# Order of the k and q products, the way to the triangular inverses, and the squares of q in a gated DeltaNet layer

## The chip, the core and the metric

The kernel runs on one core of one Trainium2 chip, in one launch. The metric is the device time of that launch in microseconds (us), median of three runs. The core's engines run at the same time, each through its own list of instructions in a fixed order, and wait for one another by semaphores: TensorE (PE in the profile; PEld is its loading of weights) multiplies into PSUM, VectorE (DVE) and ScalarE (ACT) work element by element, GpSimd (POOL) does a few odd operations, and SyncE (SP) issues most of the DMA transfers.

## The reference

One layer on x of shape (1, 256, 2048), float32. It has two parallel token mixers behind one input projection, an output projection, and a gated MLP.

```python
h = rmsnorm(x, norm_mix_w)
q, k, v, z, b_raw, a_raw, p_in, g_a, g_b = split(h @ w_in)
q, k, v = split(silu(causal_dwconv(concat([q, k, v]), conv_qkv_w)))   # 4 taps
q = l2norm(q per head) * HEAD_DIM ** -0.5;  k = l2norm(k per head)    # 16 heads of 128
o = gated_delta_rule(q, k, v, g_log, beta)                            # chunks, triangular solve
y_a = rmsnorm(o, gdn_norm_w) * silu(z)
y_b = (causal_multiscale_pool(p_in) @ pool_w per group) * pool_scale
x = x + (sigmoid(g_a) * y_a + sigmoid(g_b) * y_b) @ w_out
h = rmsnorm(x, norm_ffn_w)
gate, up = split(h @ w_up)
x = x + (gelu(causal_dwconv(gate, conv_ffn_w) + conv_ffn_b) * up) @ w_down
return rmsnorm(x, norm_final_w)
```

l2norm divides by the root of a sum of squares over a head's 128 channels. The kernel leaves q unscaled in the products and brings the sum of squares of q into the final scale of o: that is what "squares of q" means below.

## The kernel before

**Long products.** Every big product is float32, made of three products of rounded parts: a weight tile `raw` of 128 x 1024 comes by DMA; ScalarE rounds it to the high half `whi` (line 141 of the listing, L141), VectorE subtracts to get the low half `wlo` (L149); `gemm_a` (L168) then issues, for each of two rows of 128 inputs and each of two halves of the 256 tokens, x-high by `whi` (L179), x-low by `whi` (L180) and x-high by `wlo` (L181). Each of these is a product 128 x 512. A projection of 512 columns takes 8 weight tiles, 96 such products. `raw` has four buffers, `whi` and `wlo` three each, and weights are made two tiles ahead (`AHEAD`). The result stands in PSUM in a tile of the pool `psm`, which has two buffers; other PSUM tiles come from `psg`, with four.

**Groups.** The mixers run over four groups g of 512 columns, that is four heads. Before the change a group issues its long products in this order: k, q, v, p (input of the pool), g_b, the pool's small product (24 products), z, g_a. The eight weight streams are listed in the same order in `srcs`. The very first k product is done apart, while x is still being loaded.

**What follows each product.** `evict` (L552) scales the PSUM tile into `ev` on ScalarE (L557, two instructions); `ev` has one buffer. `conv_silu` (L597) turns `ev` with eight small TensorE products (`turned`, L224), scales on ScalarE (L608), adds three shifted taps on VectorE (L611), and applies silu (L614, L615) into `kq`. v goes out to DRAM (`vrow`), and comes back three times shifted as `mv`; VectorE multiplies with the taps and adds (L588, L589). The gates are a tanh on ScalarE (L871) that VectorE combines with z (L882, L884, L886). Such work is put in the list `later`, which is emptied at the second weight tile of the next long product.

**The gated delta rule.** `gdn` (L619) is a generator. After each six long products `side()` takes one step of it, so its small instructions are put between the long ones. It makes the products of k and q with themselves and their decays (L645 to L683), sends the diagonal blocks of 32 through DRAM (`cdd`) into `lb` so that all blocks can be inverted side by side, idles for `WAIT` = 5 steps, and inverts them by forward substitution on VectorE (L709 to L711, 31 steps, in `tb`). The inverses go back through DRAM (`tbd`) into `TT`, are turned by blocks (L730), and are joined into larger inverses (L743 to L772). Then come the recurrence over the chunks (L778 to L789), the outputs (`po`: L796, L798, L799), the squares of q summed by 16 products with q's squares as weights and a column of ones (L804, waited for by L812), the squares of o (L809, L810), the power on GpSimd (L814), and the scaled output (L816, L819). `gated` multiplies it with z and adds the pool's part (L890, L891), `mixed` turns the result and splits it into halves for the output projection (L903, L904).

**Order.** A scheduler places the instructions on each engine from the program order, its estimate of when operands and buffers are free, and priorities; each engine then works strictly through its list. Two places are tied by hand (`issue_after`, at the first group). The lists of the changed program can be read as well as those of the program before: where the text says "in the changed order", it is from them.

Of the kernel before, what the change touches and what calls it, by code (L numbers as in the profile page):

```python
# [7 lines left out]
F32 = mybir.dt.float32  # L8
F32R = mybir.dt.float32r
I32 = mybir.dt.int32  # L10
AF = mybir.ActivationFunctionType
ALU = mybir.AluOpType

P = 128
S = 256
D = 2048
NH = 16
KD = D // P
DFF = 5632
KF = DFF // P  # L20
EPS = 1e-6
# [3 lines left out]
C_Q, C_K, C_V, C_Z = 0, 2048, 4096, 6144  # L25
C_B, C_P, C_GA, C_GB = 8192, 8224, 10272, 12320
B0 = 32
NR = P // B0
AHEAD = 2
WAIT = 5  # L30


@with_exitstack
def kernel(
# [20 lines left out]
    nc = tc.nc  # L55
    mm = nc.tensor.matmul
# [10 lines left out]
    def nm(s):  # L67
        cnt[0] += 1
        return f"{s}_{cnt[0]}"

    def pg(shape=(P, 512)):
        return psg.tile(list(shape), F32, tag="g", name=nm("psg"))


    def cols(w, base, nk):
        return [w[c * 256 : (c + 1) * 256, base : base + 512].rearrange("(k p) f -> p k f", p=P)
                for c in range(nk // 2)]

    srcs = []
    for g in range(4):  # L80
        for base in (C_K, C_Q, C_V, C_P, C_GB):
            srcs += cols(w_in[0], base + 512 * g, KD)
            if g == 0 and base == C_K:
                srcs += [w_in[0, c * 1024 : (c + 1) * 1024, C_B : C_B + P].rearrange("(k p) f -> p k f", p=P)
                         for c in range(2)]
        srcs += cols(pool_w[0, g], 0, 4)
        for base in (C_Z, C_GA):
            srcs += cols(w_in[0], base + 512 * g, KD)
    outw = [cols(w_out[0], 512 * c, KD) for c in range(4)]
# [76 lines left out]
    later = []  # L166
# [62 lines left out]
    ones = cpool.tile([P, P], F32, name="ones")  # L229
    nc.gpsimd.memset(ones, 1.0)  # L230
    ident = cpool.tile([P, P], F32, name="ident")
# [17 lines left out]
    mp = mix.__enter__()  # L249
# [183 lines left out]
    for cq in range(4):  # L433
        pr = slice(32 * cq, 32 * cq + 32)
# [17 lines left out]
    nc.vector.tensor_tensor(id2, ident[:64, 0:32], ident[:64, 32:64], op=ALU.add)  # L452


    pba = pg([P, 2, S])
    for c in range(2):
        hi, lo = weights()
        for kk in range(8):
            k = 8 * c + kk
# [137 lines left out]
    def conv_silu(e, kind, g, dst):  # L597

        pts = turned(e)
        y = mp.tile([P, 4, S], F32, tag="cy", bufs=2, name=nm("cy"))  # L600
        for f in range(4):
            r = kind * 16 + 4 * g + f
            gs = pts[f // 2][:, f % 2, :]

            def w(j):
                return cqw[:, j * 48 + r : j * 48 + r + 1]

            nc.scalar.activation(y[:, f, :], gs, AF.Copy, scale=w(3))  # L608
            for j in (2, 1, 0):
                s = 3 - j  # L610
                nc.vector.scalar_tensor_tensor(y[:, f, s:], gs[:, : S - s], w(j), y[:, f, s:],  # L611
                                               op0=ALU.mult, op1=ALU.add)
        th = mp.tile([P, 4, S], F32, tag="th", name=nm("th"))
        nc.scalar.activation(th, y, AF.Tanh)  # L614
        k_conv.append(nc.vector.scalar_tensor_tensor(dst, th, 1.0, y, op0=ALU.add, op1=ALU.mult).ins)  # L615
# [3 lines left out]
    def gdn(g, kq, vt, conv, res):  # L619
# [79 lines left out]
        for cq in range(4):  # L699
            nc.sync.dma_start(lb[32 * cq : 32 * cq + 32], cdd.rearrange("q (r j) i -> (q r) j i", j=B0))  # L700
        yield
        for _ in range(WAIT):
            yield
        tb = mp.tile([P, 8, B0], F32, tag="tb", name=nm("tb"))
        tmp = mp.tile([P, 8, B0], F32, tag="tmp", name=nm("tmp"))
        nc.vector.tensor_copy(tb, idb)
        for j in range(B0 - 1):
# [15 lines left out]
        for h in range(4):  # L723
            for t in range(2):
                nc.scalar.activation(vt[:, t, h, :], vt[:, t, h, :], AF.Copy, scale=nk[:, t, h : h + 1])
        for _ in range(WAIT - 3):
            yield
        for r in range(NR):
            rs = slice(B0 * r, B0 * (r + 1))
            nc.vector.transpose(Ta[rs, :, rs], TTa[rs, :, rs])  # L730
# [50 lines left out]
        pr = pg([P, 4, P])  # L781
# [6 lines left out]
            mm(pw[:, h, :], TT[h // 2][:, 1, h % 2, :], vt[:, 1, h, :], start=True, stop=True)  # L788
        nc.scalar.copy(w2, pw)  # L789
        yield  # L790

        q2 = kq[:, :, 1, :]
        nc.scalar.activation(q2, q2, AF.Square)
        po = [pg([P, 4, P]) for t in range(2)]
        for h in range(4):
            mm(po[0][:, h, :], ga0[:, h, 256:384], w1[:, h, :], start=True, stop=True)  # L796
# [1 line left out]
            mm(po[1][:, h, :], ga0[:, h, 384:512], w1[:, h, :], start=True, stop=False)  # L798
            mm(po[1][:, h, :], ga1[:, h, P : 2 * P], w2[:, h, :], start=False, stop=True)  # L799
        yield  # L800
        pn = pg([P, 2, 4])
        for t in range(2):
            for h in range(4):
                mm(pn[:, t, h : h + 1], q2[:, h, t * P : (t + 1) * P], ones[:, 0:1], start=True, stop=True)  # L804
        ro = mp.tile([P, 2, 4], F32, tag="ro", name=nm("ro"))
        so = mp.tile([P, 2, 4], F32, tag="so", name=nm("so"))
        for t in range(2):
# [1 line left out]
            nc.scalar.activation(o2, po[t], AF.Square, scale=float(P) ** -0.5)  # L809
            nc.vector.tensor_reduce(so[:, t, :], o2, axis=mybir.AxisListType.X, op=ALU.add)  # L810
        yield
        nc.vector.tensor_scalar(ro, pn, EPS * P, EPS * EPS * P, op0=ALU.mult, op1=ALU.add)  # L812
        nc.vector.tensor_tensor(ro, ro, so, op=ALU.add)
        nc.gpsimd.tensor_tensor(ro, ro, epsx[:, 0:1].unsqueeze(2).to_broadcast([P, 2, 4]), op=ALU.pow)  # L814
        for t in range(2):
# [4 lines left out]
        yield  # L820
        res.append(on)

    for g in range(4):
        kq = mp.tile([P, 4, 2, S], F32, tag="kq", bufs=1, name=nm("kq"))
        for kind, dst in ((1, kq[:, :, 0, :]), (0, kq[:, :, 1, :])):
            ps = ps_k0 if kind == 1 and g == 0 else gemm_a(xh, xl, KD)
            e = evict(ps)
            later.append(lambda e=e, kind=kind, g=g, dst=dst: conv_silu(e, kind, g, dst))

        vt = mp.tile([P, 2, 4, P], F32, tag="vt", name=nm("vt"))  # L830
        vt2 = vt.rearrange("p t h d -> p t (h d)")
        res = []
        later.append(lambda g=g, kq=kq, vt=vt, res=res: side_work.__setitem__(0, gdn(g, kq, vt, v_conv(g, vt), res)))
        v_taps(g)
        if g == 0:
            def after_k(k_conv=k_conv[0]):
                with tc.issue_after(last_pow[0]), tc.issue_after(k_conv):
                    fixed_parts()

            later.append(after_k)  # L840
        e = evict(gemm_a(xh, xl, KD), rsh)
        nc.sync.dma_start(vrow[g, SH : SH + S, :].rearrange("(t p) d -> p t d", p=P), e)
        later.append(lambda e=e, g=g, vt2=vt2: v_moved(e, g, vt2))


        win = WINDOWS[g]
        psb = scales(g)
        ps = gemm_a(xh, xl, KD)
        e = evict(ps)
        phi = mtile(g, [P, 4, S], F32R, nm("phi"))  # L850
        plo = mtile(4 + g, [P, 4, S], F32R, nm("plo"))

        def pooled(e=e, g=g, phi=phi, plo=plo):
            for f2 in range(2):
                pt = pg([P, 2, S])
                for ff in range(2):
                    fs = slice((2 * f2 + ff) * P, (2 * f2 + ff + 1) * P)
                    mm(pt[:, ff, P:S], e[:, 1, fs], bands[:, g, P + PAD : NB], start=True, stop=False,
                       skip_group_check=True)
                    mm(pt[:, ff, 0 : P + PAD], e[:, 0, fs], bands[:, g, 0 : P + PAD], start=False, stop=True,  # L860
                       skip_group_check=True)
                fs = slice(2 * f2, 2 * f2 + 2)
                nc.scalar.copy(phi[:, fs, :], pt)
                nc.vector.tensor_tensor(plo[:, fs, :], pt, phi[:, fs, :].bitcast(F32), op=ALU.subtract)

        later.append(pooled)

        def gate(ps, tag):
            th = mp.tile([P, 2, 512], F32, tag=tag, name=nm("gate"))
            for t in range(2):  # L870
                nc.scalar.activation(th[:, t, :], ps[:, t, :], AF.Tanh, scale=rsh[:, t : t + 1])  # L871
            return th

        tb = gate(gemm_a(xh, xl, KD), "th")
        ps = gemm_a(lambda k, t: phi[:, k, t * P : (t + 1) * P], lambda k, t: plo[:, k, t * P : (t + 1) * P], 4)
        yb = mp.tile([P, 2, 512], F32, tag="yb", name=nm("yb"))
        nc.vector.tensor_tensor(yb, ps, psb.unsqueeze(1).to_broadcast([P, 2, 512]), op=ALU.mult)
        nc.vector.scalar_tensor_tensor(yb, tb, 1.0, yb, op0=ALU.add, op1=ALU.mult)

        ps = gemm_a(xh, xl, KD)  # L880
        sz = mp.tile([P, 2, 512], F32, tag="sz", name=nm("sz"))
        nc.vector.scalar_tensor_tensor(sz, gate(ps, "th"), 1.0, ps, op0=ALU.add, op1=ALU.mult)  # L882
        ta = gate(gemm_a(xh, xl, KD), "th")
        nc.vector.scalar_tensor_tensor(sz, ta, 1.0, sz, op0=ALU.add, op1=ALU.mult)  # L884
        sz4 = sz.rearrange("p t (h d) -> p (t h) d", h=4)
        nc.vector.tensor_tensor(sz4, sz4, gwb.unsqueeze(1).to_broadcast([P, 8, P]), op=ALU.mult)  # L886

        def gated(sz=sz, res=res, yb=yb):
            drain()
            nc.vector.tensor_tensor(sz, res[0].rearrange("p t h d -> p t (h d)"), sz, op=ALU.mult)  # L890
            nc.vector.tensor_tensor(sz, sz, yb, op=ALU.add)  # L891

        if g < 3:
            gated()
        mh = mtile(g, [P, 4, S], F32R, f"mhi{g}")
        ml = mtile(4 + g, [P, 4, S], F32R, f"mlo{g}")
        mhi.append(mh)
        mlo.append(ml)

        def mixed(sz=sz, mh=mh, ml=ml):  # L900
            for f2, pt in enumerate(turned(sz)):
                fs = slice(2 * f2, 2 * f2 + 2)
                nc.scalar.copy(mh[:, fs, :], pt)  # L903
                nc.vector.tensor_tensor(ml[:, fs, :], pt, mh[:, fs, :].bitcast(F32), op=ALU.subtract)  # L904

        if g < 3:
            later.append(mixed)
# [174 lines left out]
```

## Time and profile before

| | us |
|---|---|
| median of three runs | 1575.46 (1575.41 to 1575.91) |
| the profiled execution | 1577.65 |
| its span, first to last instruction | 1575.9 |
| mixer, four groups of about 177 us each | from about 36 to 744 |
| output projection, MLP, final norm | from about 744 on |

The profile's rows give a start, a duration, the engine, the line, the operation, the names `out<-in` and shapes; `xN` says how many instructions a row holds. In square brackets stands the idle time of the engine ahead of the row and what ended it. Durations of products overlap, as TensorE is pipelined: what a product costs is the distance between two starts. In tables by line, the columns after the shapes are the busy time in us, the mean of one in ns, and the idle time of the engine ahead of these instructions. In the list of waits, a row names who waited for whom: us in total, how often, and the longest.

### The profile page before, as it was taken

What the parts mean: (1) busy time and instruction counts of PE and PEld (TensorE: products, weight loads), DVE (VectorE), ACT (ScalarE), POOL (GpSimd) and SP (SyncE); (2) the same over time, 40 slices, a digit from 0 to 9 for tenths busy, and PEclk for the clock granted to TensorE, in tenths of its full rate; (3) what the DMA queues carried; (4) which work ended last, traced back from release to release, by engine and by line L of the source; (5) the groups of instructions that cost most, each with busy time, mean ns of one, the idle gap of its engine ahead of it and who ended that gap; (6) DMA issues with size and microseconds to landing.
All of it is one profiled execution on the core that took longest, in us unless ns stands there. A gap on an engine that the chain in (4) does not pass through costs nothing.

```text
span 1575.9 us, 21328 instructions
## 1 busy us (share of the span) xinstructions
PE 1563.6 (99%) x8078; PEld 1314.0 (83%) x8078; DVE 1067.4 (68%) x1625; ACT 745.1 (47%) x956; POOL 45.1 (3%) x69
## 2 busy tenths in 40 slices
PE   9999999999999999999999999999999999999997
PEld 8877888788878888788888888888888888888886
DVE  6897848795788757796555667766766677444544
ACT  6554436444545445444454544444444445334443
POOL 2110000000000000000000000000000000000000
PEclk9999999999999999999999999999999999999999
DMA  8676757676667756666566666666666666666662
GB/s 274 196 227 188 203 147 214 191 218 170 184 203 200 204 147 201 198 209 178 191 197 184 189 188 187 187 188 188 186 191 191 190 188 207 199 196 205 202 222 92
DMA packets 168230, 304.23 MB, mean 193 GB/s; under 512 B 19235, under 2 KB 22835, under 8 KB 167999
## 3 DMA queue, kind: packets, MB, share of 16 engines
q1 hardware_dynamic: 165104, 297.84, 63.7%
q10 hardware_dynamic: 3022, 5.03, 1.0%
q8 instruction: 63, 1.03, 0.3%
q14 instruction: 41, 0.33, 0.1%
HBM read 297.56 MB, written 5.27 MB: 192 GB/s over the span
## 4 chain that ended last, share of the span: by engine, by line
PE 94%; DMA 2%; DVE 2%; issue 2%; SPq 0%; ACT 0%; POOL 0%; POOLq 0%; DVEq 0%
PE psm L181 13%; PE psm L179 13%; PE psm L180 13%; PE psm L203 10%; PE psg L203 10%; PE psg L204 5%; PE psm L204 5%; PE psg L995 2%; PE psg L996 2%; PE psg L997 2%; PE psm L995 2%; PE psm L996 2%; PE psm L997 2%; PE psm L310 1%; DMA mv<-vrow 1%
## 5 line engine op out<-in xcount | busy, mean ns | idle before, releaser
L149 DVE TENSOR_TENSOR wlo<-raw,whi 128x1024 fp32r<-128x1024 f32 x522 | 637.5, 1223 | 385.0 <-ACT whi L141 377.5
L141 ACT CAST whi<-raw 128x1024 fp32r<-128x1024 f32 x524 | 550.6, 1053 | 715.5 <-PE psm L180 312.2
L181 PE MATMUL psm<-wlo,xhl 128*128 128x512 f32 x864 | 340.5, 394 | 1.8 <-DVE wlo L149 1.8
L179 PE MATMUL psm<-whi,xhl 128*128 128x512 f32 x864 | 339.0, 392 | 0.0
L180 PE MATMUL psm<-whi,xhl 128*128 128x512 f32 x864 | 337.9, 391 | 0.0
L203 PE MATMUL psm<-fhl,whi 128*128 128x512 f32 x704 | 246.2, 396 | 0.0
L203 PE MATMUL psg<-fhl,whi 128*128 128x512 f32 x704 | 238.0, 394 | 0.0
L204 PE MATMUL psm<-fhl,wlo 128*128 128x256 f32 x704 | 194.4, 279 | 0.0
L181 PEld LDWEIGHTS psm<-wlo,xhl 128*128 128x128 f32 x864 | 162.2, 188 | 36.6 <-DVE wlo L149 3.8
L180 PEld LDWEIGHTS psm<-whi,xhl 128*128 128x128 f32 x864 | 162.3, 188 | 33.4
L179 PEld LDWEIGHTS psm<-whi,xhl 128*128 128x128 f32 x864 | 162.3, 188 | 32.8 <-issue 0.2
L204 PE MATMUL psg<-fhl,wlo 128*128 128x256 f32 x704 | 178.7, 279 | 0.0
L203 PEld LDWEIGHTS psm<-fhl,whi 128*128 128x128 f32 x704 | 131.4, 188 | 30.5
L203 PEld LDWEIGHTS psg<-fhl,whi 128*128 128x128 f32 x704 | 129.2, 188 | 24.2
L204 PEld LDWEIGHTS psg<-fhl,wlo 128*128 128x128 f32 x704 | 132.5, 188 | 6.9
L204 PEld LDWEIGHTS psm<-fhl,wlo 128*128 128x128 f32 x704 | 132.5, 188 | 1.1
L995 PE MATMUL psg<-whi,hhi 128*128 128x512 f32 x168 | 65.5, 390 | 0.0
L996 PE MATMUL psg<-whi,hlo 128*128 128x512 f32 x168 | 65.4, 389 | 0.0
L995 PE MATMUL psm<-whi,hhi 128*128 128x512 f32 x168 | 65.4, 389 | 0.0
L996 PE MATMUL psm<-whi,hlo 128*128 128x512 f32 x168 | 65.4, 389 | 0.0
L997 PE MATMUL psm<-wlo,hhi 128*128 128x512 f32 x168 | 65.4, 389 | 0.0
L997 PE MATMUL psg<-wlo,hhi 128*128 128x512 f32 x168 | 59.0, 389 | 0.0
(259 smaller groups left out, 1523.7 us busy)
## 6 DMA issues: line engine op xcount, KB each, us to landing
raw<-in_w_in_dram SPq DMA_DIRECT2D x224, 512.0 KB, 4.2
raw<-in_w_up_dram SPq DMA_DIRECT2D x176, 512.0 KB, 3.8
raw<-in_w_down_dram SPq DMA_DIRECT2D x88, 512.0 KB, 4.4
raw<-in_w_out_dram SPq DMA_DIRECT2D x32, 512.0 KB, 4.1
mv<-vrow SPq DMA_DIRECT2D x12, 512.0 KB, 5.8
taps<-in_conv_qkv_w_dram SPq DMA_DIRECT2D x16, 256.0 KB, 5.1
raw<-in_pool_w_dram SPq DMA_DIRECT2D x8, 512.0 KB, 5.1
vrow<-ev SPq DMA_DIRECT2D x4, 512.0 KB, 2.7
```

The lines of the kernel that those rows point to most:

```text
L141: nc.scalar.copy(hi, raw)
L149: nc.vector.tensor_tensor(lo, raw, hi.bitcast(F32), op=ALU.subtract)
L179: mm(ps[:, t, :], lh(k, t), hi[:, kk, :], start=(k == 0), stop=False)
L180: mm(ps[:, t, :], ll(k, t), hi[:, kk, :], start=False, stop=False)
L181: mm(ps[:, t, :], lh(k, t), lo[:, kk, :], start=False, stop=(k == nk - 1))
L203: mm(ps[f], hi[:, kk, fs], rhl(k), start=(k == 0), stop=False, skip_group_check=True)
L204: mm(ps[f][:, 1, :], lo[:, kk, fs], rhl(k)[:, 0, :], start=False, stop=(k == nk - 1), skip_group_check=True)
L310: mm(ps_k0[:, t, :], part(k, t), w[:, kk, :], start=(k == 0 and w is hi and part is xh), stop=(k == KD - 1 and w is lo))
L995: mm(acc[c][t], lh(k, t), hi[:, kk, :], start=(k == 0), stop=False)
L996: mm(acc[c][t], ll(k, t), hi[:, kk, :], start=False, stop=False)
L997: mm(acc[c][t], lh(k, t), lo[:, kk, :], start=False, stop=(k == KF - 1))
```

## The change

* k and q of group g+1 are computed in group g, after the pool's product and ahead of z and g_a. Only the first group computes its own. The weight streams are listed accordingly. The taps of v (`v_taps`) move into `later`.
* Ahead of the inverses nine steps are idled (`WAIT + LATE`), not five; the two idle steps behind v's scaling go. `tb` gets two buffers.
* The square of q is taken when the blocks have been sent, not after the recurrence. VectorE turns the squares by 32 x 32 blocks into `qx` and adds over 32, into `qp` (128 x 32); one product with `sel` (four copies of a 32 x 32 identity, stacked and repeated) adds the four blocks of each head, and four small scalings on 32 partitions each read the result. `sel` is made once at the start.

```diff
--- before.py
+++ after.py
@@ -28,6 +28,7 @@
 NR = P // B0
 AHEAD = 2
 WAIT = 5
+LATE = 4
 
 
 @with_exitstack
@@ -77,13 +78,16 @@
                 for c in range(nk // 2)]
 
     srcs = []
+    srcs += cols(w_in[0], C_K, KD)
+    srcs += [w_in[0, c * 1024 : (c + 1) * 1024, C_B : C_B + P].rearrange("(k p) f -> p k f", p=P) for c in range(2)]
+    srcs += cols(w_in[0], C_Q, KD)
     for g in range(4):
-        for base in (C_K, C_Q, C_V, C_P, C_GB):
+        for base in (C_V, C_P, C_GB):
             srcs += cols(w_in[0], base + 512 * g, KD)
-            if g == 0 and base == C_K:
-                srcs += [w_in[0, c * 1024 : (c + 1) * 1024, C_B : C_B + P].rearrange("(k p) f -> p k f", p=P)
-                         for c in range(2)]
         srcs += cols(pool_w[0, g], 0, 4)
+        if g < 3:
+            for base in (C_K, C_Q):
+                srcs += cols(w_in[0], base + 512 * (g + 1), KD)
         for base in (C_Z, C_GA):
             srcs += cols(w_in[0], base + 512 * g, KD)
     outw = [cols(w_out[0], 512 * c, KD) for c in range(4)]
@@ -450,6 +454,12 @@
 
     id2 = mp.tile([64, 32], F32, name="id2")
     nc.vector.tensor_tensor(id2, ident[:64, 0:32], ident[:64, 32:64], op=ALU.add)
+
+
+    sel = mp.tile([P, 4, 32], F32, name="sel")
+    nc.vector.tensor_reduce(sel[:, 0, :], ident.rearrange("p (b i) -> p i b", b=4), axis=mybir.AxisListType.X,
+                            op=ALU.add)
+    nc.vector.tensor_copy(sel[:, 1:4, :], sel[:, 0:1, :].to_broadcast([P, 3, 32]))
 
 
     pba = pg([P, 2, S])
@@ -699,9 +709,12 @@
         for cq in range(4):
             nc.sync.dma_start(lb[32 * cq : 32 * cq + 32], cdd.rearrange("q (r j) i -> (q r) j i", j=B0))
         yield
-        for _ in range(WAIT):
+
+        q2 = kq[:, :, 1, :]
+        nc.scalar.activation(q2, q2, AF.Square)
+        for _ in range(WAIT + LATE):
             yield
-        tb = mp.tile([P, 8, B0], F32, tag="tb", name=nm("tb"))
+        tb = mp.tile([P, 8, B0], F32, tag="tb", bufs=2, name=nm("tb"))
         tmp = mp.tile([P, 8, B0], F32, tag="tmp", name=nm("tmp"))
         nc.vector.tensor_copy(tb, idb)
         for j in range(B0 - 1):
@@ -723,8 +736,14 @@
         for h in range(4):
             for t in range(2):
                 nc.scalar.activation(vt[:, t, h, :], vt[:, t, h, :], AF.Copy, scale=nk[:, t, h : h + 1])
-        for _ in range(WAIT - 3):
-            yield
+
+        qx = mp.tile([P, 4, S], F32, tag="dec0", name=nm("qx"))
+        nc.vector.transpose(qx, q2)
+        yield
+        qp = mp.tile([P, 32], F32, tag="qp", name=nm("qp"))
+        nc.vector.tensor_reduce(qp, qx.rearrange("p h (c j) -> p (h c) j", j=32), axis=mybir.AxisListType.X,
+                                op=ALU.add)
+        yield
         for r in range(NR):
             rs = slice(B0 * r, B0 * (r + 1))
             nc.vector.transpose(Ta[rs, :, rs], TTa[rs, :, rs])
@@ -788,9 +807,6 @@
             mm(pw[:, h, :], TT[h // 2][:, 1, h % 2, :], vt[:, 1, h, :], start=True, stop=True)
         nc.scalar.copy(w2, pw)
         yield
-
-        q2 = kq[:, :, 1, :]
-        nc.scalar.activation(q2, q2, AF.Square)
         po = [pg([P, 4, P]) for t in range(2)]
         for h in range(4):
             mm(po[0][:, h, :], ga0[:, h, 256:384], w1[:, h, :], start=True, stop=True)
@@ -798,10 +814,8 @@
             mm(po[1][:, h, :], ga0[:, h, 384:512], w1[:, h, :], start=True, stop=False)
             mm(po[1][:, h, :], ga1[:, h, P : 2 * P], w2[:, h, :], start=False, stop=True)
         yield
-        pn = pg([P, 2, 4])
-        for t in range(2):
-            for h in range(4):
-                mm(pn[:, t, h : h + 1], q2[:, h, t * P : (t + 1) * P], ones[:, 0:1], start=True, stop=True)
+        pn = pg([P, 4, 2, 4])
+        mm(pn.rearrange("p h t c -> p (h t c)"), sel.rearrange("p b i -> p (b i)"), qp, start=True, stop=True)
         ro = mp.tile([P, 2, 4], F32, tag="ro", name=nm("ro"))
         so = mp.tile([P, 2, 4], F32, tag="so", name=nm("so"))
         for t in range(2):
@@ -809,7 +823,10 @@
             nc.scalar.activation(o2, po[t], AF.Square, scale=float(P) ** -0.5)
             nc.vector.tensor_reduce(so[:, t, :], o2, axis=mybir.AxisListType.X, op=ALU.add)
         yield
-        nc.vector.tensor_scalar(ro, pn, EPS * P, EPS * EPS * P, op0=ALU.mult, op1=ALU.add)
+        for c in range(4):
+            pr = slice(32 * c, 32 * c + 32)
+            nc.vector.tensor_scalar(ro[pr], pn[pr, :, :, c].rearrange("p h t -> p t h"), EPS * P, EPS * EPS * P,
+                                    op0=ALU.mult, op1=ALU.add)
         nc.vector.tensor_tensor(ro, ro, so, op=ALU.add)
         nc.gpsimd.tensor_tensor(ro, ro, epsx[:, 0:1].unsqueeze(2).to_broadcast([P, 2, 4]), op=ALU.pow)
         for t in range(2):
@@ -820,18 +837,22 @@
         yield
         res.append(on)
 
-    for g in range(4):
+    def keys(g):
+
         kq = mp.tile([P, 4, 2, S], F32, tag="kq", bufs=1, name=nm("kq"))
         for kind, dst in ((1, kq[:, :, 0, :]), (0, kq[:, :, 1, :])):
             ps = ps_k0 if kind == 1 and g == 0 else gemm_a(xh, xl, KD)
             e = evict(ps)
-            later.append(lambda e=e, kind=kind, g=g, dst=dst: conv_silu(e, kind, g, dst))
-
+            later.append(lambda e=e, kind=kind, dst=dst: conv_silu(e, kind, g, dst))
+        return kq
+
+    kq = keys(0)
+    for g in range(4):
         vt = mp.tile([P, 2, 4, P], F32, tag="vt", name=nm("vt"))
         vt2 = vt.rearrange("p t h d -> p t (h d)")
         res = []
         later.append(lambda g=g, kq=kq, vt=vt, res=res: side_work.__setitem__(0, gdn(g, kq, vt, v_conv(g, vt), res)))
-        v_taps(g)
+        later.append(lambda g=g: v_taps(g))
         if g == 0:
             def after_k(k_conv=k_conv[0]):
                 with tc.issue_after(last_pow[0]), tc.issue_after(k_conv):
@@ -877,6 +898,8 @@
         nc.vector.tensor_tensor(yb, ps, psb.unsqueeze(1).to_broadcast([P, 2, 512]), op=ALU.mult)
         nc.vector.scalar_tensor_tensor(yb, tb, 1.0, yb, op0=ALU.add, op1=ALU.mult)
 
+        if g < 3:
+            kq = keys(g + 1)
         ps = gemm_a(xh, xl, KD)
         sz = mp.tile([P, 2, 512], F32, tag="sz", name=nm("sz"))
         nc.vector.scalar_tensor_tensor(sz, gate(ps, "th"), 1.0, ps, op0=ALU.add, op1=ALU.mult)
```

## The prediction

> **What bounds the kernel now.** I read the page's engine shares and its chain of waits first, then the busy time by stage, then the stops of TensorE one by one.
>
> ```profile
> span 1575.9 us, 21328 instructions
> PE 1563.6 (99%) x8078; PEld 1314.0 (83%) x8078; DVE 1067.4 (68%) x1625; ACT 745.1 (47%) x956; POOL 45.1 (3%) x69
> ...
> PE 94%; DMA 2%; DVE 2%; issue 2%; SPq 0%; ACT 0%; POOL 0%; POOLq 0%; DVEq 0%
> ```
>
> TensorE is busy 99% of the span and holds 94% of the chain that ends last. So an edit counts by what it takes off or puts on TensorE's instruction stream, or by a stop of TensorE. The four groups of the mixer, by windows of 177 us (columns: window, length, busy time of PE, PEld, DVE, ACT, POOL, then granted clock, DMA share, GB/s):
>
> ```profile
> 36.00:213.00 177.00, 175.72 (x872) 143.35 (x871) 139.90 (x278) 82.86 (x109) 13.18 (x23) 1.00 0.69 200
> 213.00:390.00 177.00, 176.42 (x902) 145.13 (x901) 133.63 (x233) 84.80 (x112) 7.58 (x7) 1.00 0.66 191
> 390.00:567.00 177.00, 177.00 (x907) 146.25 (x907) 133.90 (x234) 86.11 (x113) 7.10 (x7) 1.00 0.68 192
> 567.00:744.00 177.00, 175.75 (x900) 144.68 (x899) 132.24 (x225) 84.63 (x112) 6.92 (x7) 1.00 0.64 189
> ```
>
> Only 1.28, 0.58, 0 and 1.25 us are not busy, at full clock: removing stops can win little. VectorE has about 43 us free in each group, as an average. The stops themselves, in TensorE's timeline:
>
> ```profile
> 135.42 0.39 PE L179 MATMUL psm<-whi,phi 128*128 128x512 f32 x1
> 135.65 0.39 PE L180 MATMUL psm<-whi,plo 128*128 128x512 f32 x1
> 137.31 0.50 PE L181 MATMUL psm<-wlo,phi 128*128 128x512 f32 x1 [1.28 <-DVE wlo L149]
> ...
> 313.31 0.39 PE L180 MATMUL psm<-whi,xhl 128*128 128x512 f32 x1
> 314.24 0.50 PE L181 MATMUL psm<-wlo,xhl 128*128 128x512 f32 x1 [0.53 <-DVE wlo L149]
> ...
> 649.83 0.39 PE L180 MATMUL psm<-whi,xhl 128*128 128x512 f32 x1
> 650.80 0.50 PE L181 MATMUL psm<-wlo,xhl 128*128 128x512 f32 x1 [0.58 <-DVE wlo L149]
> ...
> 658.86 0.39 PE L180 MATMUL psm<-whi,xhl 128*128 128x512 f32 x1
> 659.92 0.50 PE L181 MATMUL psm<-wlo,xhl 128*128 128x512 f32 x1 [0.67 <-DVE wlo L149]
> ```
>
> A product is issued each 0.23 us (135.42 to 135.65). What the interval has above that is lost: 1.44, 0.70, 0.74 and 0.83 us, 3.7 in all. Each waits for the low half of a weight tile (L149). VectorE was itself held by transfers:
>
> ```profile
> DVE tmp L709 <- DMA lb<-cdd: 15.2, 4, 6.2
> DVE mv L588 <- DMA mv<-vrow: 9.1, 5, 2.8
> ```
>
> **The squares of q.** L804 sums the squares with 16 one-column products a group:
>
> ```profile
> 224.26 1.84 PE L804 MATMUL psg<-ones,kq 128*128 128x1 f32 x16
> 225.97 0.48 PE L181 MATMUL psm<-wlo,xhl 128*128 128x512 f32 x1
> ```
>
> They hold TensorE for 225.97 − 224.26 = 1.71 us, 0.107 each. One product with `sel` as weights, in two passes of about the same 0.107 us, takes 0.21: 4 × (1.71 − 0.21) = **−6.0**. A pass of 0.23, as long as a 512-column one, would make it −5.0. VectorE gets the block turns and a sum instead. From these rows
>
> ```profile
> L730 DVE STREAM_TRANSPOSE T<-TT 32x256 f32<-32x256 f32 x16 | 7.0, 436 | 7.0 <-DMA TT<-tbd 6.6
> L756 DVE STREAM_TRANSPOSE TT<-T 32x128 f32<-32x128 f32 x16 | 4.8, 303 | 0.5
> L810 DVE TENSOR_REDUCE so<-o 128x4 f32<-128x512 f32 x8 | 5.5, 686 | 14.7 <-ACT o L809 14.7
> ```
>
> 128 more columns of turning cost 0.133 us, so 1024 columns about 1.2; the reduction of 1024 by the rate of L810 also about 1.2. In the changed order both stand ahead of L730, where VectorE waited 7.0 us for TT, 1.75 a group; so 2.4 − 1.75 = 0.65 a group can remain, 2.6 in all if no weight tile is ahead. I take 0, the tiles being up to two ahead. The square itself (ScalarE) only moves in the program; four small scalings in place of one cost VectorE 3 × 0.17. `sel` is made in the opening stretch, well under 1 us, before any group.
>
> **Fewer interruptions.** Each block of side products costs TensorE 0.1 us when it returns to the long product (0.32 from 243.60 to 243.92 below, against 0.23). The changed order has 89 such blocks for 94: **−0.5**.
>
> **The longer way to the inverse.** L709 waits 15.2 us for `lb` in the row above. Between the last L683 and the first L709 VectorE's order has 3, 3, 4, 5 low halves before and 3, 4, 4, 4 after. So the first group's stop of 1.44 stays as it is, although four steps are added; the second group gets the 4 of the third, whose window has no stop. The other three stops (0.70 + 0.74 + 0.83 = 2.27) lie in a v and p stretch that is arranged anew. I let them go but charge 0.4 for new small ones: **−1.9**. Bounds: −2.3, if none comes, and 0, if each is replaced by its like. In SP's order the weight tiles follow their use as before, and none comes to stand behind a longer wait of `vrow`, `cdd` or `lb`: 0 for the moved transfers, up to 0.7 a group (the 0.67 and 0.70 above) if one did. The second buffer of `tb` only ends a wait of VectorE that no product waits for.
>
> **Next k and q ahead of z: the stop at z's end.** Now k(g+1), q(g+1), z and the gate follow each other. The order shows what this does: `ev` has one buffer, and k's turning (L224) stands behind the last L799 of the group's mixer, at z's end, with none of z's products left. The gate's first product needs the PSUM buffer of q; its eviction (L557) needs `ev`, which k's turning must have read, and on ScalarE it stands behind two L608. How long this takes is seen before at 242.81:
>
> ```profile
> 242.81 1.04 PE L224 MATMUL psg<-ident,ev 128*128 128x128 f32 x8
> 243.60 0.48 PE L181 MATMUL psm<-wlo,xhl 128*128 128x512 f32 x1
> 243.92 0.39 PE L179 MATMUL psm<-whi,xhl 128*128 128x512 f32 x1
> ...
> 243.53 0.86 ACT L608 ACTIVATE cy<-psg,cqw 128x256 f32<-128x256 f32 x2
> 244.26 1.29 ACT L557 ACTIVATE ev<-psm,rs 128x512 f32<-128x512 f32 x2
> ```
>
> From the first turn to the end of the eviction: 244.26 + 1.29 − 242.81 = 2.74 us. There the long product went on at 243.60, as it had another buffer. Here it can't: 2.74 less 0.87 for the eight turns = 1.9 us, three times, **+5.7**. Bounds: 1.3, if the eviction starts as soon as the last turn is through, and 2.6, if a row as long as L810's (0.69), the square L809 ahead of it, is still on ScalarE. The Trainium skill, "Perfetto Trace Analysis", section Optimizing Tensor Performance, holds that product groups which rotate through PSUM banks have one group's evacuation overlapped by the next one's products. The trace agrees at 243.60; by that rule alone the sum would be without these 5.7.
>
> In the first group L783 and L788 also become neighbours; before, 23 long products stood between them. L788 then waits for L784 (0.69, row below): 0.39 for L783's last product + 0.69 + 0.1 for two signals (an estimate) − 0.23 = **+0.95** (0 to 1.2).
>
> **The stop between the gate and the next v.** v's first product takes z's buffer, which L882 frees. L882 follows the tanh (L871), which on ScalarE now stands behind the high half of v's second tile; that tile's buffer comes free 14 issues before the gate ends.
>
> ```profile
> L141 ACT CAST whi<-raw 128x1024 fp32r<-128x1024 f32 x524 | 550.6, 1053 | 715.5 <-PE psm L180 312.2 <-PE psm L203 127.7 <-PE psg L203 90.7
> L871 ACT ACTIVATE gate<-psm,rsh 128x512 f32<-128x512 f32 x24 | 15.2, 682 | 0.1
> L882 DVE SCALAR_TENSOR_TENSOR sz<-gate,psm 128x1024 f32<-128x1024 f32 x4 | 4.9, 1218 | 0.0
> L784 DVE TENSOR_TENSOR vt<-vt,psg 128x512 f32<-128x512 f32 x4 | 2.7, 686 | 4.6 <-PE psg L783 4.6
> L903 ACT CAST mhi<-psg 128x512 fp32r<-128x512 f32 x8 | 4.3, 590 | 0.3
> ```
>
> That product's end 0.39 after issue, 1.05 + 1.29 (two tanh, as the two L557 above) + 1.22 + 0.25 for four signals (an estimate) = 4.2, less 14 × 0.227 = 3.2: 1.0 us, three times, **+3.0**. Bounds 0 (the tanh in time) and 2, if VectorE comes 1 us late from q's convolution.
>
> **The last group's end.** It has no k and q after it, and its inverse starts later. Before, 62 long products lay between the last L799 and the turning of `sz`; in the changed order 34, or 7.7 us. The work between them, from the first group:
>
> ```profile
> 227.62 0.39 PE L799 MATMUL psg<-w,ga 128*128 128x128 f32 x2
> ...
> 228.68 0.69 DVE L810 TENSOR_REDUCE so<-o 128x4 f32<-128x512 f32 x1 [0.96 <-ACT o L809]
> 231.31 0.36 DVE L816 TENSOR_SCALAR ro<-ro,rsq 128x4 f32<-128x4 f32 x2 [1.75 <-POOL ro L814]
> 232.80 1.28 DVE L819 TENSOR_TENSOR on<-psg,ro 128x512 f32<-128x512 f32 x2
> 235.53 1.22 DVE L890 TENSOR_TENSOR sz<-on,sz 128x1024 f32<-128x1024 f32 x1
> 236.78 1.22 DVE L891 TENSOR_TENSOR sz<-sz,yb 128x1024 f32<-128x1024 f32 x1
> ```
>
> 238.00 − 227.62 = 10.4 us with two low halves (1.22 each) in it; I take 9.7, as one is half covered: a stop of 2.0. Bounds 0.2 (both low halves ahead) and 2.7. Then L903 (0.59) and the low half behind it wait with no products between, where there were ten: 0.8 (0 to 1.3). Together **+2.8**.
>
> **Sum:** −6.0 − 0.5 − 1.9 + 5.7 + 0.95 + 3.0 + 2.8 = +4.05 us. The profiled execution took 1577.65 (span 1575.9 and 1.7 around it), so 1581.7; it stood 2.2 above the median, so the median goes from 1575.46 to **1579.5**, 0.26% slower.
>
> **Rivals.** *No wait at z's end or at v* (faster). If the last L799 came some us before z ends, the turning and eviction would run under z's products; the point from which it decides is 2.74 us, or 12 products, of z left at k's turning. Then, without 5.7, 0.95 and 3.0, −6.0 − 0.5 − 1.9 + 2.8 = −5.6: 1570. For it: the four windows hide nearly everything now. Against: TensorE's order is fixed, and no product of z is left there. *The tanh comes in time*, and one other wait is small: +4.05 − 3.0 − 1 = 0: 1575.5, no difference. *VectorE becomes the bound in the gate's product.* Into its 96 × 0.227 = 21.8 us fall both convolutions and the group's tail:
>
> ```profile
> L611 DVE SCALAR_TENSOR_TENSOR cy<-psg,cqw,cy 128x255 f32<-128x255 f32 x32 | 14.2, 473 | 0.0
> ```
>
> 24 of these make 11.4; two L615 2.4 (as the other rows of 1024), seven low halves 8.6, L810 and L819 2.7, small ones 1.0: 26.1 us. With the stop ahead there are 23.7, so 2.4 us come late, three times: 1586.7. Against it: weights are two tiles (2 × 2.7 us of products) ahead, which takes up as much. The Trainium skill ("TensorE: Matmul & The Clock Gate", HAM oscillation) adds that an idle window of some 3.4 us halves the clock; the trace's longest stop, 1.28 us, left it at 1.00, and no row here shows a longer one. By that page such stops would cost about 1.7 us more each, an estimate.
>
> **Chances.** Forecast 0.46 (its own range 1577.5 to 1582), VectorE's bound 0.18, tanh in time 0.22, faster 0.14. About 0.2% (3.2 us) is what a measurement can tell. Slower takes nearly all of the forecast and VectorE's case, 0.59; within 0.2% the rest of the forecast and the tanh's case, 0.27; faster 0.14. The range 1572 to 1586 leaves out most of the faster case and the far end of VectorE's.
>
> **What would show it.** L804 gone and two passes of 0.1 in its place; a stop of about 1.9 us at the gate's first product in three groups, released by ScalarE's L557; one of about 1 us at v's first product, released by the former L882; about 2 us before the last turning of `sz`; the stop at 137.3 unchanged. Wrong would be: the gate's products following z's at 0.3 us, or low halves late inside the gate's product by more than 1 us.

## The result, and the profile after

| | us |
|---|---|
| before, median of five runs | 1575.91 (1575.41 to 1578.45) |
| after, median of five runs | 1582.72 (1582.13 to 1583.99) |
| ratio, with its 95% interval | 1.0041 (1.0029 to 1.0052) |
| profiled execution after, and its span | 1583.02, 1581.3 |

The change makes the kernel 0.4% slower: 5.4 us in the two profiled spans, 6.8 in the medians. The page after:

```profile
span 1581.3 us, 21253 instructions
PE 1561.4 (99%) x8022; PEld 1309.1 (83%) x8022; DVE 1079.7 (68%) x1647; ACT 746.3 (47%) x956; POOL 42.9 (3%) x69
...
PE 96%; DVE 1%; ACT 1%; issue 1%; DMA 1%; POOL 0%; POOLq 0%; SPq 0%; DVEq 0%
```

TensorE is busy 2.2 us less than before and the span is 5.4 longer: work has gone, and more waiting has come. The work that went, in the groups by line after (L818 is the one product per group in two passes; L741 and L744 are the turning and the adding on VectorE):

```profile
L818 PE MATMUL psg<-qp,sel 128*128 128x32 f32 x8 | 1.2, 236 | 0.0
L741 DVE STREAM_TRANSPOSE qx<-kq 128x1024 f32<-128x1024 f32 x4 | 4.9, 1236 | 0.0
L744 DVE TENSOR_REDUCE qp<-qx 128x32 f32<-128x1024 f32 x4 | 4.8, 1210 | 0.0
```

The 64 one-column passes of before (eight products a group, each in two passes) are 8 now. By the distance from each start to the next one, L804 took 6.8 us of TensorE in all and L818 takes 0.6. The two VectorE operations cost 1.2 us each, as estimated from the shorter ones.

The waiting that came, first at z's end in the first group (TensorE's timeline):

```profile
214.31 0.83 PE L802 MATMUL psg<-w,ga 128*128 128x128 f32 x6
215.93 1.16 PE L807 MATMUL psg<-vt,TT 128*128 128x128 f32 x8 [0.78 <-DVE vt L803]
...
219.60 0.39 PE L815 MATMUL psg<-w,ga 128*128 128x128 f32 x2
219.82 1.04 PE L228 MATMUL psg<-ident,ev 128*128 128x128 f32 x8
222.58 0.50 PE L183 MATMUL psm<-whi,xhl 128*128 128x512 f32 x1 [1.72 <-ACT ev L567]
```

The last L815 (L799 before) is followed at once by k's turning (L228), and the gate's first product comes 2.76 us after the first turn, released by the eviction L567. The same 1.72 stands at 405.06 and 587.62 in the next groups. Above it, L807 waits 0.78 for L803 (L788 and L784 before). Then some 24 us later, at the gate's end, with ScalarE and VectorE beside TensorE:

```profile
245.17 0.39 PE L185 MATMUL psm<-wlo,xhl 128*128 128x512 f32 x1
246.18 0.50 PE L183 MATMUL psm<-whi,xhl 128*128 128x512 f32 x1 [0.62 <-DVE sz L905]
...
242.65 1.06 ACT L145 CAST whi<-raw 128x1024 fp32r<-128x1024 f32 x1 [0.67 <-PE psm L184]
243.60 1.26 ACT L892 ACTIVATE gate<-psm,rsh 128x512 f32<-128x512 f32 x2
...
244.90 1.22 DVE L905 SCALAR_TENSOR_TENSOR sz<-gate,psm 128x1024 f32<-128x1024 f32 x1
```

The high half, two tanh, L905 (L882 before), then v: 1.01 us from product to product where 0.23 is usual, in all three groups. And at the mixer's end:

```profile
778.01 0.39 PE L185 MATMUL psm<-wlo,mhi 128*128 128x512 f32 x1
780.35 1.33 PE L228 MATMUL psg<-ident,sz 128*128 128x128 f32 x8 [1.95 <-DVE sz L914]
781.65 1.22 PE L183 MATMUL psm<-whi,mhi 128*128 128x512 f32 x2
782.67 0.63 PE L184 MATMUL psm<-whi,mlo 128*128 128x512 f32 x1
783.10 0.63 PE L185 MATMUL psm<-wlo,mhi 128*128 128x512 f32 x1
783.53 0.63 PE L183 MATMUL psm<-whi,mhi 128*128 128x512 f32 x1
783.96 0.61 PE L184 MATMUL psm<-whi,mlo 128*128 128x512 f32 x1
784.38 0.41 PE L185 MATMUL psm<-wlo,mhi 128*128 128x512 f32 x1
```

The turning of `sz` waits 1.95 us for VectorE. After that the products come 0.43 us apart, nearly double. Windows of 1 us of the same execution (the number before the last two is the granted clock) say why:

```profile
781.00:782.00 1.00, 1.00 (x5) 0.63 (x4) 0.70 (x2) 0.87 (x2) 0.00 (x0) 0.50 0.01 2
782.00:783.00 1.00, 1.00 (x3) 0.77 (x3) 0.99 (x2) 0.31 (x1) 0.00 (x0) 0.50 0.38 125
783.00:784.00 1.00, 1.00 (x4) 0.71 (x4) 0.03 (x1) 0.00 (x0) 0.00 (x0) 0.50 0.91 315
784.00:785.00 1.00, 1.00 (x5) 0.82 (x4) 0.00 (x0) 0.00 (x0) 0.00 (x0) 0.79 0.66 178
```

The clock was halved for some 3.4 us behind the stop. Of the old stops one is left, in the first group, and one is new:

```profile
107.00 0.39 PE L184 MATMUL psm<-whi,xhl 128*128 128x512 f32 x1
107.71 0.50 PE L185 MATMUL psm<-wlo,xhl 128*128 128x512 f32 x1 [0.33 <-DVE wlo L153]
...
136.64 0.39 PE L184 MATMUL psm<-whi,plo 128*128 128x512 f32 x1
137.62 0.50 PE L185 MATMUL psm<-wlo,phi 128*128 128x512 f32 x1 [0.60 <-DVE wlo L153]
```

They cost 0.49 and 0.75 us (0.71 and 0.98, less 0.227 each), where the four of before cost 3.71.

### The profile page after: what moved, and what is told of

Read it like the earlier page. It is cut to its first block, busy times and chain, and to the rows that moved or that the text cites. A ratio compares the mean times of both kernels' runs of the same rounds, so it can differ in the third digit from the quotient of the medians.

```text
span 1581.3 us, 21253 instructions
## 1 busy us (share of the span) xinstructions
PE 1561.4 (99%) x8022; PEld 1309.1 (83%) x8022; DVE 1079.7 (68%) x1647; ACT 746.3 (47%) x956; POOL 42.9 (3%) x69
## 4 chain that ended last, share of the span: by engine, by line
PE 96%; DVE 1%; ACT 1%; issue 1%; DMA 1%; POOL 0%; POOLq 0%; SPq 0%; DVEq 0%
PE psm L183 14%; PE psm L184 14%; PE psm L185 14%; PE psm L207 10%; PE psg L207 10%; PE psg L208 5%; PE psm L208 5%; PE psg L1018 2%; PE psg L1019 2%; PE psg L1020 2%; PE psm L1019 2%; PE psm L1018 2%; PE psm L1020 2%; PE psm L314 1%; PE psg L674 1%
## 5 line engine op out<-in xcount | busy, mean ns | idle before, releaser
L184 PE MATMUL psm<-whi,xhl 128*128 128x512 f32 x864 | 338.3, 392 | 0.0
L184 PEld LDWEIGHTS psm<-whi,xhl 128*128 128x128 f32 x864 | 162.2, 188 | 33.4
```

The costliest lines, as they stand in the source:

```text
L184: mm(ps[:, t, :], ll(k, t), hi[:, kk, :], start=False, stop=False)
```

## The experiments

Seven kernels, each against the kernel before on the same chip (1576.74 us there for the first four, 1576.63 for the others). Two theories stood to begin with. A is the account of the prediction, brought up to date by the profile after: every stop has its place in the order of the engines, and moving the instruction moves the stop. The rivals are given with each run.

**The squares alone.** The old lists and loops of k and q, `LATE` out, one buffer of `tb`:

```diff
-        if g < 3:
-            kq = keys(g + 1)
...
     for g in range(4):
+        kq = mp.tile([P, 4, 2, S], F32, tag="kq", bufs=1, name=nm("kq"))
+        for kind, dst in ((1, kq[:, :, 0, :]), (0, kq[:, :, 1, :])):
+            ps = ps_k0 if kind == 1 and g == 0 else gemm_a(xh, xl, KD)
...
-        for _ in range(WAIT + LATE):
+        for _ in range(WAIT):
```

> The change's new way of summing q's squares, with the old order of the k and q products and without the four added idle steps. Theory A (the account from the stops: squares -6.2, stops at z's end +5.6, before v +2.3, at the last group's end +3.8 with the clock's drop, old stops -2.5): this kernel keeps k and q behind the gate, so it has no stop at z's end or before v; in its order 42 long products lie between the last L799 and the turning of sz (62 before, 34 after), 9.5 us for a chain of 9.7 to 10.4, so a stop of 0.2 to 0.9 and no drop of the clock: before - 5.5 us, about 1570, with a range of 1568.5 to 1572. Rival B (turning and adding on VectorE costs what the products save, and the stops at z's end are paid back elsewhere): within 2 us of before.

Measured: 1572.02 us, ratio 0.9969 (0.9958 to 0.9981): faster than before by 4.7 us, and the fastest kernel of this study. At z's end and before v nothing waits. The last turning of `sz`, in TensorE's timeline:

```profile
769.45 0.39 PE L182 MATMUL psm<-wlo,mhi 128*128 128x512 f32 x1
769.68 1.03 PE L225 MATMUL psg<-ident,sz 128*128 128x128 f32 x8
771.23 0.74 PE L180 MATMUL psm<-whi,mhi 128*128 128x512 f32 x2 [0.52 <-ACT mhi L917]
772.61 0.50 PE L181 MATMUL psm<-whi,mlo 128*128 128x512 f32 x1 [0.64 <-DVE mlo L918]
```

With 42 products ahead the turning is in time; only the halves behind it (L903 and L904 before) wait, about 1.4 us. So theory A holds in the main and B falls, though the gain is 0.8 us short of A's 5.5. In the two profiled spans it is 5.4 us. The squares take 6.25 off. The stops cost about as much as before: two of the old kind are left (0.75 and 1.34 us), which with those at the end make 3.5, for 3.7. What is given back lies elsewhere: TensorE returns 96 times from small products to the long ones, for 87 times before, at about 0.1 us each, and the mixer's long stretch starts 0.46 later (36.77 for 36.31).

**The order alone.** The k and q lists of the change, the old squares, no added steps:

```diff
-        pn = pg([P, 4, 2, 4])
-        mm(pn.rearrange("p h t c -> p (h t c)"), sel.rearrange("p b i -> p (b i)"), qp, start=True, stop=True)
+        pn = pg([P, 2, 4])
+        for t in range(2):
+            for h in range(4):
+                mm(pn[:, t, h : h + 1], q2[:, h, t * P : (t + 1) * P], ones[:, 0:1], start=True, stop=True)
```

> Only the k and q products of the next group ahead of z and the first gate; the squares as before, no added idle steps, one buffer for the inverses. Theory A's stops depend on where the order puts k's turning, and in this order 11 long products (2.5 us) are left at z's end behind it in the second and third group, none in the first; 56 products lie ahead of the last turning of sz. So a stop of 1.8 at z's end in the first group, 0.3 in the two others, 0.8 before v three times, none at the end, no drop of the clock, old stops 2.5 less: before + 2 us, about 1578. Rival C (the parts add up; the order has its stops whatever the squares do): the change less its squares, 1582.7 + 6.2, about 1589.

Measured: 1582.38 us, ratio 1.0038 (1.0024 to 1.0051), between the two theories. The stop at z's end is there in the first group:

```profile
220.13 1.04 PE L228 MATMUL psg<-ident,ev 128*128 128x128 f32 x8
222.88 0.50 PE L183 MATMUL psm<-whi,xhl 128*128 128x512 f32 x1 [1.72 <-ACT ev L561]
```

In the second and third, where 11 products are left behind k's turning, there is none, and the three stops before v are there with 0.6 idle each: so the places were right. Two costs had been overlooked: L788 waits for L784 here too (0.78 idle), and so do the two halves after the last turning (0.52 and 0.64). Both parts together cost 5.4 us more than their sum (+6.3 for the same order as the change, below, against −4.7 + 5.6 = +0.9): with both, k's turning stands at the very end of z in three groups, not in one, which is 3.8 of it. The stops for low halves do not add up either: they cost 3.7 us before, 2.1 with the squares alone, 0.5 with the order alone and 2.1 with both. The second buffer of `tb` was not tried by itself.

**No added steps.** One line:

```diff
-LATE = 4
+LATE = 0
```

> The changed kernel with 0 added idle steps in place of 4. Theory A's step in the prediction (the inverse starts later, which brings the last group's end stop and L783 beside L788): the end stop of 2.1 us and the halved clock behind it go, 3.8 us less, about 1579. Rival D (the scheduler places these instructions by its own times, and idle steps move nothing; the orders on all engines are instruction for instruction the same): the same time and the same stops as the changed kernel, 1582.7 within 1 us.

Measured: 1583.0 us, ratio 1.0035 (1.0022 to 1.0049), the time of the changed kernel within 0.3 us. The lists of all five engines are the same, instruction by instruction, with 0, 4, 8 or 12 added steps. Rival D is right: the "longer way to the inverses" moves nothing. This run also gives the end stop a second time:

```profile
778.19 0.39 PE L185 MATMUL psm<-wlo,mhi 128*128 128x512 f32 x1
780.53 1.07 PE L228 MATMUL psg<-ident,sz 128*128 128x128 f32 x8 [1.95 <-DVE sz L914]
781.83 0.73 PE L183 MATMUL psm<-whi,mhi 128*128 128x512 f32 x2 [0.24 <-ACT mhi L926]
782.56 0.50 PE L184 MATMUL psm<-whi,mlo 128*128 128x512 f32 x1
782.90 0.40 PE L185 MATMUL psm<-wlo,mhi 128*128 128x512 f32 x1
783.13 0.39 PE L183 MATMUL psm<-whi,mhi 128*128 128x512 f32 x1
783.36 0.39 PE L184 MATMUL psm<-whi,mlo 128*128 128x512 f32 x1
```

The same wait of 1.95 us, and then products at the usual 0.23: here the clock stayed at 1.00. From the first turn to the second L184 it is 2.83 us here and 3.61 after the change (780.35 to 783.96). With the two products that were still slow there, the halved clock cost some 1.0 us.

**q's eviction in a buffer of its own.**

```diff
-            e = evict(ps)
+            e = evict(ps, own=kind == 0)
...
-        e = mp.tile([P, 2, 512], F32, tag="ev", bufs=1, name=nm("ev"))
+        e = mp.tile([P, 2, 512], F32, name=nm("ev"), **(dict(tag="mv") if own else dict(tag="ev", bufs=1)))
```

> The changed kernel with q's eviction in the buffer of mv, so that it need not wait for k's turning out of ev. Theory A: the three stops of 1.8 at z's end go, and the 0.8 of L803 in the first group; the order also moves 42 products ahead of the last turning, so the end stop falls to 0.2 to 0.9 and the clock stays at 1.00 (3.3 less). But z's tanh now stands behind q's convolution, and the stop before v can grow from 0.8 to as much as 3 each. So 9 less and 0 to 7 more: 1574 to 1581. Rival E (it is not ev but ScalarE's queue that holds the gate): stops at z's end as before, 1582.

Measured: 1608.07 us, ratio 1.0198 (1.0184 to 1.0212). Both theories missed. The three stops at z's end are gone, as A says, but v's first product waits:

```profile
245.83 0.39 PE L185 MATMUL psm<-wlo,xhl 128*128 128x512 f32 x1
256.97 0.79 PE L183 MATMUL psm<-whi,xhl 128*128 128x512 f32 x1 [10.75 <-DVE sz L905]
...
252.04 1.06 ACT L624 ACTIVATE th<-cy 128x1024 f32<-128x1024 f32 x1 [2.17 <-DVE cy L621]
254.40 1.27 ACT L892 ACTIVATE gate<-psm,rsh 128x512 f32<-128x512 f32 x2 [1.29 <-DVE kq L625]
```

z's tanh (L892) starts when q's convolution has used up its own tanh (L625): both write the buffer `th`, of which there is one. The stop is 10.75 us in the first group and 5.9 in the two others, and a halved clock goes with each. A fourth stop, of 3.56 us at 105.34 in the first group, also with a halved clock, is a wait for a low half, which stands on VectorE behind L598; L598 had waited 3.77 us for `mv`, the buffer that q's eviction borrows here, which is the likely reason but was not tried apart. So not all of the loss is due to `th`. I had seen the order and put 0 to 3 us on it; I had not followed who holds `th`.

**z's tanh in a buffer of its own.** This asks for the cause of the stop before v.

```diff
-        nc.vector.scalar_tensor_tensor(sz, gate(ps, "th"), 1.0, ps, op0=ALU.add, op1=ALU.mult)
+        for t in range(2):
+            nc.scalar.activation(sz[:, t, :], ps[:, t, :], AF.Tanh, scale=rsh[:, t : t + 1])
+        nc.vector.scalar_tensor_tensor(sz, sz, 1.0, ps, op0=ALU.add, op1=ALU.mult)
```

> The changed kernel with z's tanh written into sz, not into the buffer th, which it shares with the convolutions of k and q. Theory A: z's tanh and L882 no longer wait for q's convolution, so the stop of 0.8 before v goes in all three groups (2.3); the gate's product then takes z's buffer and waits for tanh and L882, 2.5 us in place of 1.8. The order has 15 products before the last turning: an end stop of 6.3 to 7 in place of 2.1 and the halved clock. 1583 - 2.3 + 2.1 + 4.5 + 1 = 1588. Rival G (the stop before v is the high half ahead of the tanh on ScalarE, as the prediction said, not the shared buffer): the stops before v stay at 0.8: 1590.

Measured: 1583.01 us, ratio 1.0038 (1.0025 to 1.0052). No product waits before v any more, which is A and not G: the shared `th` is what put the tanh so late on ScalarE. The stops at z's end are gone as well, which I had not expected: tanh and L882 now run under the 4 us of small products (L807 to L815) at z's end, from 214.44 to 217.57 in the first group, and the gate's product follows at 219.61 in z's buffer without waiting for q's eviction. What this won is lost at the end:

```profile
770.72 0.39 PE L185 MATMUL psm<-wlo,mhi 128*128 128x512 f32 x1
777.40 1.94 PE L228 MATMUL psg<-ident,sz 128*128 128x128 f32 x8 [6.29 <-DVE sz L916]
```

**15 products before the last turning.** The squares alone, with another buffer for the turned squares, which moves the last group's tail:

```diff
-        qx = mp.tile([P, 4, S], F32, tag="dec0", name=nm("qx"))
+        qx = mp.tile([P, 4, S], F32, tag="mv", name=nm("qx"))
```

> The squares alone (old order of k and q), with the turned squares in the buffer of mv in place of dec0. By this the order has 15 long products between the last L799 and the last turning of sz, where squares_alone has 42. Theory A (that distance sets the end stop, and a stop beyond about 2 us brings the halved clock): 15 x 0.227 = 3.4 us for a chain of 9.7 to 10.4, a stop of 6.3 to 7 before the turning, then about 3.4 us at clock 0.50, which cost 1.7, against none in squares_alone: squares_alone + 7 to 9, about 1580. Rival F (the chain is run faster when little stands between, and the end stop is a matter of VectorE's low halves): a stop under 4 us, about 1575.

Measured: 1577.2 us, ratio 1.0004 (0.9995 to 1.0013), 5.2 above the squares alone. A's stop came as worked out, F's did not:

```profile
767.80 0.39 PE L182 MATMUL psm<-wlo,mhi 128*128 128x512 f32 x1
774.47 1.94 PE L225 MATMUL psg<-ident,sz 128*128 128x128 f32 x8 [6.29 <-DVE sz L905]
```

6.67 us less 0.23 is 6.4, where 6.3 to 7 was expected, and the clock was at 0.50 from about 772.1 to 778.9. The total rose by 5.2 and not by 7 to 9, since the waits for the halves (1.4 in squares_alone) do not show behind the slow clock, and the stops for low halves are 0.7 less. So the distance ahead of the last turning sets the end stop.

**Thirty added steps.** `LATE = 30`, the rest as in the change.

> The changed kernel with 30 added idle steps in place of 4. In the program the mixer's last PSUM tiles then come after the turning of k, and in the order k's turning moves from z's end to z's first third in all three groups. Theory A (the stop at z's end is k's turning coming behind the mixer's tail, as the PSUM tiles of psg rotate in the order of the program): the three stops of 1.8 go and the 0.8 of L803; 42 products lie before the last turning, so the end costs 1.3 as in squares_alone, with no drop of the clock, in place of 2.1 and up to 1.7. The stop before v is open: z's tanh stands behind q's convolution, 0 to 4 a group. So 1583 - 6.2 - 2 and 0 to 8 more: 1572 to 1582, my value 1576. Rival E (ScalarE's queue or VectorE sets the stop at z's end, wherever k is turned): 1582 or more, with stops at z's end.

Measured: 1578.45 us, ratio 1.0009 (1.0000 to 1.0018), 4.3 us below the changed kernel and 1.8 above the kernel before. The stops at z's end and the one of L803 are gone, so A holds and E falls: at thirty steps the mixer's last small tiles are laid out after k's turning, and the turning comes early in z. Before v, the first group waits longer, and the clock falls with it (0.50 from 244.9 to 251.7); the second group does not wait there, the third 0.62:

```profile
242.51 0.39 PE L185 MATMUL psm<-wlo,xhl 128*128 128x512 f32 x1
246.23 0.80 PE L183 MATMUL psm<-whi,xhl 128*128 128x512 f32 x1 [3.33 <-DVE sz L905]
```

## Why the prediction was right, point by point

The forecast was +4.05 us with slower at 0.59; 6.8 came in the medians and 5.4 in the profiled spans. The terms, from distances between starts in the profile after:

| term | forecast | measured |
|---|---|---|
| squares of q | −6.0 | −6.25 |
| fewer interruptions | −0.5 | +0.4 |
| old stops, less new small ones | −1.9 | −2.5 |
| z's end, three groups | +5.7 | +5.7 (1.99 − 0.1 each) |
| L788 waits for L784 | +0.95 | +0.96 |
| before v, three groups | +3.0 | +2.3 |
| last group's end | +2.8 | +2.8 (2.11 and 0.72) |
| the halved clock | not in the sum | +1.0 |
| sum | +4.05 | +3.4, and +4.4 with the clock |

* *Squares.* Right in size, and squares_alone shows it by itself. That VectorE would hide the turning was right too.
* *The sum.* Without the clock the terms come to +3.4, near the forecast partly by luck: interruptions came 0.9 dearer, old stops 0.6 and the stops before v 0.7 cheaper. The same terms for the run without added steps (no halved clock, −1.6 for the old stops) make +4.3, and its span is 4.5 above that of before.
* *Interruptions.* There are five blocks fewer, as read off the lists (82 returns to the long products for 87), but what they cost above 0.227, stops and slow clock left out, is about 12.9 us for 12.5. The term was wrong by 0.9 us.
* *z's end.* The mechanism and its size were read off the old boundary (2.74 us from first turn to the end of the eviction) and came within 0.1. That k's PSUM tiles come behind the mixer's in the program is a cause that thirty_steps speaks for; z_own_tanh shows that the stop can be avoided by freeing z's buffer in time.
* *The longer way.* This step failed in its reason: the prediction said the last group's "inverse starts later" by it. The added steps move no instruction at all. What moves the last group's tail is not settled: 62 products lay ahead of the last turning before, 56 with the order alone, 42 with the squares alone, 34 with both, 15 where only the turned squares' buffer differs. It depends on buffers through the scheduler; by which rule was not tried. That the first group's stop stays was half right: 0.75 for 1.44. These stops vary from execution to execution: with the same order, the run without added steps has 1.13 there and 0.97 for the new one, where the change has 0.75 and 0.49.
* *L788.* The two signals, put at 0.1 as an estimate, took 0.09 in the first group: 0.04 from L783's end to L784, 0.05 from L784's end to L788.
* *Before v.* 0.77 for 1.0 each. The prediction named the high half ahead of the tanh; z_own_tanh puts the shared buffer `th` behind that.
* *The end.* 2.11 for 2.0, and 0.7 for 0.8 for the halves. The clock was not in the sum; it stood only beside it, as a rule. That no row showed a longer idle overlooks the end of the trace of before: TensorE's last product ended at 1567.79, and the clock was at 0.50 from 1571.59.
* *The rest.* Of the remaining 5.4 − 4.4 = 1.0 us, 0.5 is a later start of the mixer's long stretch (36.78 for 36.31), which the run without added steps, in the same order, does not show (36.26); the other half is spread over intervals of small products. The medians differ by 1.4 more than the spans of these two executions; the kernel before alone spread over 3 us in its five runs.

Of the rivals, VectorE as the bound did not come: no low half was late inside the gate's product. The rule of rotating PSUM banks (the Trainium skill, "Perfetto Trace Analysis", Optimizing Tensor Performance), by which 5.7 us would have been missing, did not hold where one buffer outside PSUM (`ev`, `th`) ties the evacuations together.

## What to carry to other kernels

A product that is moved takes its evictions along: look for every single buffer that these share with what now stands beside them (`ev`, `th` here), and for the order in which small PSUM tiles are laid out in the program. Where a scheduler orders the engines, compare the lists before costing an edit: four idle steps did nothing, and a change of one buffer's tag moved the end by 27 products. Try the parts alone: the squares by themselves beat both kernels.

## What the runs showed of the hardware

A stop of TensorE can cost more than itself. Behind the 1.95 us wait for `sz` the clock was granted at 0.50 in one execution and stayed at 1.00 in another one with the same order; stops of 1.72 us never brought it, those of 3.3 us and more always did (thirty_steps, own_ev, end_at_15, z_own_tanh). The halved stretches last 3.4 us or two, three or four times that, by the clock's record in the traces: 781.0 to 784.4 after the change, 772.1 to 778.9 with 15 products, 773.2 to 783.4 with z's own tanh, 248.6 to 262.3 in own_ev.

The same record tells why one stop hits and its like misses. In each trace all changes of the clock are a whole number of 3.413 us apart, over the full-speed stretches too: after the change, 227 of them lie between the first rise at 6.18 and the fall at 781.00. The stop lies whole inside one such window after the change, and is cut in two by a boundary at 779.52 in the run without added steps (window, length, busy time of PE, and so on as before):

```profile
777.59:781.00 3.41, 1.46 (x10) 1.02 (x9) 3.38 (x4) 1.04 (x1) 0.00 (x0) 1.00 0.57 186
```

```profile
776.11:779.52 3.41, 2.47 (x11) 1.69 (x10) 3.38 (x5) 1.66 (x2) 0.00 (x0) 1.00 0.56 166
779.52:782.94 3.42, 2.17 (x12) 1.49 (x13) 3.12 (x4) 1.08 (x2) 0.00 (x0) 1.00 0.47 162
```

TensorE is idle for 1.95 us of the first window, and for 0.94 and 1.25 of the two others. Of some 4100 such windows at full clock in the nine traces, the ends of the kernels included, all 17 with 1.95 us idle or more were followed by 0.50, and none with 1.76 or less was. What counts, as far as these traces go, is therefore the idle time inside one window. Where the boundaries fall differed between the two executions of the same order (first rise at 6.18 and at 4.70).

The Trainium skill, "TensorE: Matmul & The Clock Gate", section "What's actually happening", has a window of 3413 ns, free-running against the kernel, and a halved clock after an idle one. The lengths agree, and so does it that the same stop can hit or miss; but a window with 1.95 us idle was enough here, not only an idle one, and there the trace decides.
